# Two more pairs by seven: the first down groups of an FFN's second and third parts, and how their weights and left sides are summed

## The chip, the cores and the metric

The kernel runs on one core of one Trainium2 chip. The metric is the device time of one execution in microseconds (us). The engines are PE (TensorE, matmuls; PEld is its weight loads), DVE (VectorE), ACT (ScalarE), POOL (GpSimd, which here mostly issues DMAs) and SP (SyncE, which issues DMAs).

## The reference

One decoder block on 256 tokens with a model width of 2048, all in float32:

```
h = h + 1/2 * SwiGLU_a(RMSNorm(h))          # FFN1
n = RMSNorm(h); P = n @ W_in                # mixer
h = h + concat(GatedDeltaNet, StickBreaking) @ W_out
h = h + 1/2 * SwiGLU_b(RMSNorm(h))          # FFN2
h = h + sigmoid(RMSNorm(h) @ W_pg) * (p @ W_pp)
out = RMSNorm(h)

def swiglu(x, w_gu, w_down):
    gate, up = jnp.split(x @ w_gu, 2, axis=-1)
    return (jax.nn.silu(gate) * up) @ w_down        # w_gu 2048 x 11264, w_down 5632 x 2048
```

Only the two FFNs are touched by the change.

## The kernel before, in words

**Three matmuls for one.** Each operand is split in a high half (a cast to fp32r) and a low half (the residual), and a float32 product is made of hi x hi, hi x lo and lo x hi. A matmul here is always 128 x 128 (the left side, loaded as weights) by 128 x 512.

**Plain pairs.** Weights come in pairs of 128-row blocks (`weight_pair`, line 70 on): SP loads `raw` (512 KB), ACT casts `whi` (L77), DVE makes `wlo` (L78). One pair serves 2 blocks x 2 token halves x 3 = 12 matmuls (L550 to L552).

**Groups.** An FFN's 5632 hidden columns are eleven blocks of 512, in three parts: `PARTS = ((0, 3), (3, 7), (7, 11))`. Part one has three gate/up groups, then two down groups; parts two and three have four and two. In the code the parts are numbered 0, 1, 2, so part two's down weights are `w_down11` in FFN1. A group accumulates into four PSUM banks: two weight blocks by two token halves (a 2 x 2 product of blocks). A down group of part two or three has eight pairs for each of its two blocks.

**By seven.** The first `ns` pairs of a group are not multiplied plainly (24 matmuls for a pair of both blocks) but by seven products of a 2 x 2 scheme with 7 multiplications, 21 matmuls for a pair. The seven products belong to the next group but run inside the group before it, one after each plain pair ("sevenths"). Their weights are sums of four quarters, loaded by POOL into four banks `R` (L279): B11, B21, B12, B22 are `(0,0)`, `(1,0)`, `(0,1)`, `(1,1)`. `all_sums` forms the sums in place, either on DVE (`add`, L307) or by an accumulating DMA from POOL (`add_loaded`, L314); ACT casts each to `shi` (L298) and DVE makes the residual `slo` (L299). Two buffers of each exist. The products run in the order `SEVEN = (0, 1, 2, 4, 3, 5, 6)` (`product`, L342 to L344); numbers 0, 4 and 6 use plain left sides, 1, 2, 3 and 5 sums of them.

**Left sides.** The left sides of a down group are the hidden values `hTh`, `hTl`. `down_input` makes them after each gate/up group: `sil` is multiplied by the up product (DVE L482), transposed in squares (`tb`, L487), written to DRAM scratch (L493), read back as `tT` (L498) and split into `hTh` (ACT L504) and `hTl` (DVE L505). `halves` sums them for the products: one S of 512 columns for a pair (L456), four small operations of 128 columns (L462), then the cast `Sh` (ACT L464) and residual `Sl` (DVE L465). For parts two and three this is put in a lane after the sixth seventh of the second last gate/up group, one pair at a time.

**Order.** The program is written in the order of the lanes and groups; a scheduler reorders it within its own model, except for instructions marked `keep_in_program_order`. `next_weights` asks for weights two steps ahead. `last`, handed to `down_input` for a part's last block, is the number of steps (plain pairs) before the split of `tT` is issued.

Of the kernel before, what the change touches and what calls it, by code (L numbers as in the profile page):

```python
# [10 lines left out]
F32 = mybir.dt.float32  # L11
F32R = mybir.dt.float32r
AF = mybir.ActivationFunctionType
ALU = mybir.AluOpType
# [13 lines left out]


NS = 4  # L30
NS_DOWN = tuple(3 if i1 - i0 == 4 else 2 for i0, i1 in PARTS)


SEVEN = (0, 1, 2, 4, 3, 5, 6)


W_IN_ORDER = (2, 0, 4, 3, 1, 5, 8, 10, 12, 9, 11, 13, 6, 7)
# [9 lines left out]
def block_kernel(ctx, tc, a, out):  # L47
# [200 lines left out]
    class Group:  # L248
# [8 lines left out]
        def __init__(self, kind, part, src, quarters, ns, bank, nb=0):  # L257
            self.kind, self.part, self.src, self.ns, self.nb, self.bank = kind, part, src, ns, nb, bank
            self.quarters, self.raw, self.first = quarters, {}, False
            self.last = part == len(PARTS) - 1  # L260
            self.banks = self.follower = None
            self.plain = [(b, g) for b in range(2) for g in range(ns, len(src[0]))]
            if kind == "dn" and nb == 0:

                self.plain.sort(key=lambda x: x[1] >= len(src[0]) - 2)
            elif kind == "behind":

                self.plain.sort(key=lambda x: x[1] // 2)
            self.sums = self.all_sums()
# [11 lines left out]
        def loads(self, last=None):  # L281


            free = [last.home[q] for q in ((1, 0), (0, 1), (1, 1), (0, 0))] if last else ["R0", "R1", "R2", "R3"]
            self.queue = nc.gpsimd if last else nc.sync
            use = (0, 0), (0, 1), (1, 1), (1, 0)
            self.home = dict(zip(use, free))
            return [("load", lambda q=q: self.load(*q)) for q in use]

        def all_sums(self):  # L290

            fp = current[0]

            def halved(j, b):
                w = self.raw[j, b]
                hi = fp.tile([P, NS, NB], F32R, tag="shi", name="shi", bufs=2)[:, 0:self.ns]
                lo = fp.tile([P, NS, NB], F32R, tag="slo", name="slo", bufs=2)[:, 0:self.ns]
                keep(nc.scalar.copy(hi, w))  # L298
                nc.vector.tensor_tensor(out=lo, in0=w, in1=hi, op=ALU.subtract)  # L299
                return hi, lo  # L300

            def keep(ins):

                return tc.keep_in_program_order(ins) if self.first == "2" else ins

            def add(x, y):
                keep(nc.vector.tensor_tensor(out=self.raw[x], in0=self.raw[x], in1=self.raw[y], op=ALU.add))  # L307

            def add_loaded(x, y):


                if self.first:
                    return add(x, y)
                nc.gpsimd.dma_start(out=self.raw[x], in_=self.quarters[y[1]][y[0]], accum_op=ALU.add)  # L314
# [39 lines left out]
    def plan(n):  # L354
# [9 lines left out]
        for p, (i0, i1) in enumerate(PARTS):  # L364
            for i in range(i0, i1):
                plain = PLAIN[n]
                if i < plain:
                    src = [([a[f"w_gu{n}0"][2 * i + b][g] for g in range(KD // 2)], None) for b in range(2)]
                else:
                    src = [sources("w_gu" + n, 2 * (i - plain) + b) for b in range(2)]  # L370
                groups.append(Group("gu", p, [x[0] for x in src], [x[1] for x in src], NS if i >= plain else 0,
                                    len(groups) % 2))
            for nb in (0, 2):
                src = [sources(f"w_down{n}{p}", nb + b) for b in range(2)]
                groups.append(Group("dn", p, [x[0] for x in src], [x[1] for x in src], NS_DOWN[p], len(groups) % 2, nb))
# [47 lines left out]
    def halves(kind, his, los, ns, wait=0, at_once=2):  # L423


        for _ in range(wait):
            yield
# [12 lines left out]

        sides[kind] = side

        for g0 in range(0, ns, at_once):
            n = min(at_once, ns - g0)
            k0 = 2 * (g0 % 2)
            hi, lo = (x[g0 // 2][:, k0:k0 + 2 * n] for x in (his, los))
            keep = lambda ins: ins
            if g0 == 2 and n == 1:

                keep = tc.keep_in_program_order  # L450
                yield
            if n == 2:
                x = fp.tile([P, 2 * NB], F32, tag="sil", name="S")
            else:
                x = act.tile([P, NB], F32, tag="nat", name="S", bufs=4)
            keep(nc.vector.tensor_tensor(out=x, in0=hi.bitcast(F32).rearrange("p k x -> p (k x)"),  # L456
                                         in1=lo.bitcast(F32).rearrange("p k x -> p (k x)"), op=ALU.add))
            xv = x.rearrange("p (g j t y) -> p g j t y", g=n, j=2, t=2)
            a11, a12, a21, a22 = (xv[:, :, j, t, :] for t in range(2) for j in range(2))
            for o, y, z, op in ((a22, a21, a22, ALU.subtract), (a21, a11, a21, ALU.subtract),  # L460
                                (a11, a22, a11, ALU.subtract), (a12, a11, a12, ALU.add)):
                nc.vector.tensor_tensor(out=o, in0=y, in1=z, op=op)  # L462
            sx = [y[:, g0:g0 + n].rearrange("p g j t y -> p (g j t y)") for y in (sh, sl)]
            nc.scalar.copy(sx[0], x)  # L464
            nc.vector.tensor_tensor(out=sx[1], in0=x, in1=sx[0], op=ALU.subtract)  # L465
            if not g0 % 2 + n == 1 or g0 + n == ns:
                yield

    def ffn(n, nT, r, scale, next_norm, stat):
        xs = picker(*nT)  # L470
        late = callable(r)
        with tc.tile_pool(name="ffn", bufs=1) as fp:
            hTh, hTl = [], []

            def down_input(u, sil, th, tl, last):

# [24 lines left out]
                for t in range(2):  # L501
                    hi, lo = (x[:, :, t * P:(t + 1) * P].rearrange("p j (q y) -> p q j y", q=4) for x in (th, tl))
                    tv = tT[:, :, t].rearrange("p q (j y) -> p q j y", j=4)
                    keep(nc.scalar.copy(hi, tv))  # L504
                    keep(nc.vector.tensor_tensor(out=lo, in0=tv, in1=hi, op=ALU.subtract))  # L505

            def gated(g):
                sil = fp.tile([P, 2, NB], F32, tag="sil", name="sil")
# [7 lines left out]
            for group, todo in ffn_plan[n]:  # L516
# [5 lines left out]
                if dn and group.nb and not group.last:  # L522
                    lanes.add(1, halves("gu", *nT, NS))
                elif dn and group.nb and group.follower:
                    lanes.add(1, halves("behind", *nxt, NS_BEHIND, 4))
                elif not dn and group.follower.kind == "dn" and not group.part:
                    lanes.add(1, halves("dn", hTh[i0:], hTl[i0:], NS_DOWN[group.part]))
# [4 lines left out]
                for kind, one in todo:  # L532
                    if kind == "seventh":
                        follower = group.follower
                        follower.product(SEVEN[one])
                        if group.part and not dn and one == 5 and follower.kind == "gu" and \
                                follower.follower.kind == "dn":
                            p = PARTS[group.part][0]
                            lanes.add(1, halves("dn", Later(hTh, p), Later(hTl, p), NS_DOWN[group.part], 0, 1))
                        continue  # L540
                    b, g = one
                    whi, wlo = next_weights()
# [29 lines left out]
                    else:  # L572
# [776 lines left out]
def _layout(i):  # L1349
# [7 lines left out]
    for n in "12":  # L1357
# [4 lines left out]
        _parted(m, f"w_gu{n}", b[2 * PLAIN[n]:], NS)  # L1362
        b = _blocks(f[f"ffn{n}_w_down"][0])
        for p, (i0, i1) in enumerate(PARTS):
            _parted(m, f"w_down{n}{p}", b[:, 2 * i0:2 * i1], NS_DOWN[p])
# [32 lines left out]
```

## Time and profile before

| | us |
|---|---|
| three runs | 1946.11, 1944.25, 1944.34 |
| median | 1944.34 |
| profiled execution | 1945.28 |
| its span | 1943.6 |

The time of an execution is 1.7 us more than its span. In the profile's rows, a group of instructions has its busy time and the mean of one in ns; idle time in front of it is named with what ended it. In the table of stretches each engine has its busy time and the number of its instructions in that stretch; matmul ends are modelled, so PE's own busy time is always full there, and what it lost is seen from the number of its weight loads. In FFN1 part two's third gate/up group runs from 300.16 to 340.96 us, its last from 340.96 to 377.18, its two down groups from 377.18 to 465.21.

### The profile page before, as it was taken

Reading aid. Unit: us, or ns where it says so; the run is one execution under the profiler, and the core shown is the slowest. Engines: PE = TensorE matmul, PEld = TensorE weight load, DVE = VectorE, ACT = ScalarE, POOL = GpSimd, SP = SyncE. Lnnn points to the kernel's source line nnn. Section 1 sums busy time; section 2 is a strip of 40 time slices with the busy share of each in tenths; the row PEclk is TensorE's granted clock in tenths of the full one; section 3 lists DMA queues with packets and bytes.
Section 4 is the critical chain, followed back from the end, with each engine's and each line's share of the span. In section 5 each row is a group of like instructions: output and inputs, shape, how many; then the busy total and the mean of one; then the engine's idle time right before and its main releaser. Section 6 shows DMA issues by size and latency. Waiting matters only on the chain.

```text
span 1943.6 us, 24163 instructions
## 1 busy us (share of the span) xinstructions
PE 1928.1 (99%) x8884; PEld 1594.0 (82%) x8884; DVE 1570.4 (81%) x1703; ACT 1164.1 (60%) x1362; POOL 148.4 (8%) x226
## 2 busy tenths in 40 slices
PE   9999999999999999999999999999999999999998
PEld 7888888888888888878788888888888888888886
DVE  7879878997789766797856579899888987888865
ACT  6656666666666557664555456566556755657654
POOL 0010110000010000010100000010000100001000
PEclk9999999999999999999999999999999999999999
DMA  8778898888888765556565776788888987989764
GB/s 307 269 236 282 252 293 285 237 288 249 280 285 242 228 218 171 176 169 211 161 213 159 244 283 231 226 281 289 248 275 241 327 264 244 271 237 314 234 214 143
DMA packets 144182, 475.05 MB, mean 244 GB/s; under 512 B 19648, under 2 KB 47296, under 8 KB 129856
## 3 DMA queue, kind: packets, MB, share of 16 engines
q1 hardware_dynamic: 107200, 302.16, 44.4%
q0 software_dynamic: 25920, 160.44, 30.2%
q10 hardware_dynamic: 10944, 10.91, 1.8%
q8 instruction: 69, 1.13, 0.2%
q14 instruction: 49, 0.40, 0.1%
HBM read 451.44 MB, written 22.02 MB: 244 GB/s over the span
## 4 chain that ended last, share of the span: by engine, by line
PE 92%; DVE 5%; DMA 2%; issue 1%; ACT 0%; POOL 0%; SPq 0%; POOLq 0%; DVEq 0%; ACTq 0%
PE d L550 5%; PE d L552 5%; PE d L551 5%; PE u L551 5%; PE u L552 5%; PE u L550 5%; PE g L343 5%; PE g L342 5%; PE g L344 5%; PE g L551 4%; PE g L552 4%; PE pj L112 4%; PE pj L113 4%; PE pj L114 4%; PE g L550 4%; PE d L344 3%
## 5 line engine op out<-in xcount | busy, mean ns | idle before, releaser
L77 ACT CAST whi<-raw 128x1024 fp32r<-128x1024 f32 (+1 forms) x489 | 511.3, 1049 | 401.1 <-PE pj L114 106.6
L78 DVE TENSOR_TENSOR wlo<-raw,whi 128x1024 fp32r<-128x1024 f32 (+1 forms) x489 | 592.0, 1218 | 162.9 <-ACT whi L77 161.8
L299 DVE TENSOR_TENSOR slo<-R,shi 128x2048 fp32r<-128x2048 f32 (+2 forms) x224 | 444.9, 1989 | 132.1 <-ACT shi L298 130.1
L298 ACT CAST shi<-R 128x2048 fp32r<-128x2048 f32 (+2 forms) x224 | 373.9, 1671 | 141.5 <-DVE R L307 62.7
L112 PE MATMUL pj<-whi,nTh 128*128 128x512 f32 x448 | 179.4, 401 | 0.0
L113 PE MATMUL pj<-wlo,nTh 128*128 128x512 f32 x448 | 175.2, 391 | 1.1 <-DVE wlo L78 1.1
L114 PE MATMUL pj<-whi,nTl 128*128 128x512 f32 x448 | 174.9, 390 | 0.0
L550 PE MATMUL d<-whi,hTh 128*128 128x512 f32 x448 | 174.5, 390 | 0.0
L551 PE MATMUL d<-wlo,hTh 128*128 128x512 f32 x448 | 174.4, 389 | 0.0
L552 PE MATMUL d<-whi,hTl 128*128 128x512 f32 x448 | 173.4, 389 | 0.0
L551 PE MATMUL g<-wlo,nTh 128*128 128x512 f32 x400 | 156.6, 391 | 0.6 <-DVE wlo L78 0.6
L552 PE MATMUL g<-whi,nTl 128*128 128x512 f32 x400 | 156.0, 390 | 0.0
L551 PE MATMUL u<-wlo,nTh 128*128 128x512 f32 x400 | 155.8, 389 | 0.2 <-DVE wlo L78 0.2
L552 PE MATMUL u<-whi,nTl 128*128 128x512 f32 x400 | 155.6, 389 | 0.0
L550 PE MATMUL g<-whi,nTh 128*128 128x512 f32 x400 | 155.0, 391 | 0.6 <-ACT nTh L161 0.6
L550 PE MATMUL u<-whi,nTh 128*128 128x512 f32 x400 | 153.4, 389 | 0.0
L307 DVE TENSOR_TENSOR R<-R 128x2048 f32<-128x2048 f32 (+2 forms) x68 | 135.7, 1996 | 0.1
L113 PEld LDWEIGHTS pj<-wlo,nTh 128*128 128x128 f32 x448 | 84.2, 188 | 18.9 <-DVE wlo L78 2.7
L550 PEld LDWEIGHTS d<-whi,hTh 128*128 128x128 f32 x448 | 84.1, 188 | 18.1 <-ACT hTh L504 1.0
L552 PEld LDWEIGHTS d<-whi,hTl 128*128 128x128 f32 x448 | 84.1, 188 | 17.8
L114 PEld LDWEIGHTS pj<-whi,nTl 128*128 128x128 f32 x448 | 84.1, 188 | 17.6
L551 PEld LDWEIGHTS d<-wlo,hTh 128*128 128x128 f32 x448 | 84.1, 188 | 17.4
(332 smaller groups left out, 3447.0 us busy)
## 6 DMA issues: line engine op xcount, KB each, us to landing
raw<-in_w_gu SPq DMA_DIRECT2D x199, 512.0 KB, 5.8
raw<-in_w_down SPq DMA_DIRECT2D x112, 512.0 KB, 6.4
raw<-in_w_in SPq DMA_DIRECT2D x112, 512.0 KB, 3.4
R<-in_w_gu2q POOLq DMA_DIRECT2D x54, 1024.0 KB, 8.6
R<-in_w_gu1q POOLq DMA_DIRECT2D x48, 1024.0 KB, 8.3
raw<-in_w_out SPq DMA_DIRECT2D x32, 512.0 KB, 4.3
tT<-scr SPq DMA_DIRECT2D x22, 512.0 KB, 5.8
R<-in_w_down11q POOLq DMA_DIRECT2D x12, 768.0 KB, 7.0
```

The costliest lines, as they stand in the source:

```text
L77: nc.scalar.copy(hi[:, j, :], raw[:, j, :])
L78: nc.vector.tensor_tensor(out=lo[:, j, :], in0=raw[:, j, :], in1=hi[:, j, :], op=ALU.subtract)
L112: nc.tensor.matmul(outs[t], xh[:, c], whi[:, j, :], start=st, stop=False)
L113: nc.tensor.matmul(outs[t], xh[:, c], wlo[:, j, :], start=False, stop=False)
L114: nc.tensor.matmul(outs[t], xl[:, c], whi[:, j, :], start=False, stop=sp)
L298: keep(nc.scalar.copy(hi, w))
L299: nc.vector.tensor_tensor(out=lo, in0=w, in1=hi, op=ALU.subtract)
L307: keep(nc.vector.tensor_tensor(out=self.raw[x], in0=self.raw[x], in1=self.raw[y], op=ALU.add))
L344: nc.tensor.matmul(out, xl, whi[:, g, :], start=False, stop=sp, skip_group_check=True)
L550: nc.tensor.matmul(out, xh[:, c], whi[:, j, :], start=st, stop=False, skip_group_check=True)
L551: nc.tensor.matmul(out, xh[:, c], wlo[:, j, :], start=False, stop=False, skip_group_check=True)
L552: nc.tensor.matmul(out, xl[:, c], whi[:, j, :], start=False, stop=sp, skip_group_check=True)
```

## The change

For parts two and three, the first down group takes four pairs by seven instead of three; part two's second down group too, part three's second stays at three (`NS_DOWN`). In the first down groups, the product of A12 (number 4) comes second (`SEVEN_DOWN`), its quarter B21 is loaded second, and B11 + B12 is made by an accumulating DMA where DVE did it. The left sides of the first two pairs are summed in the gate/up group before (`first_sides`) and split directly after the sixth seventh; those of pairs two and three are summed straight from `tT` in `down_input`, behind its split, and split one step later; none is put in program order by itself except those in `down_input`. `last` falls from 3 to 2 where four pairs go by seven. `halves` is cut into functions for this.

```diff
-NS_DOWN = tuple(3 if i1 - i0 == 4 else 2 for i0, i1 in PARTS)
+NS_DOWN = (2, 2), (4, 4), (4, 3)
...
+SEVEN_DOWN = (0, 4, 1, 2, 3, 5, 6)
...
+            self.seven = SEVEN_DOWN if kind == "dn" and part and nb == 0 else SEVEN
...
-            use = (0, 0), (0, 1), (1, 1), (1, 0)
+            use = ((0, 0), (0, 1), (1, 1), (1, 0)) if self.seven is SEVEN else ((0, 0), (1, 0), (0, 1), (1, 1))
...
-            for i in SEVEN:
+            for i in self.seven:
...
                 if i == 0:
-                    add((0, 0), (0, 1))
+                    (add if self.seven is SEVEN else add_loaded)((0, 0), (0, 1))
                     add_loaded((0, 1), (1, 1))
...
+            def first_sides(p0):
+                for _ in range(4):
+                    yield
+                for g in range(2):
+                    x = act.tile([P, NB], F32, tag="nat", name="S", bufs=4)
+                    sum_sides(x, hTh[p0:], hTl[p0:], g)
+                    early.append(x)
+                    yield
+
+            def later_sides(s, made):
+                yield
+                for g, x in made:
+                    split_sums(s, g, x)
...
+                if pending:
+                    s, ns = pending.pop()
+                    made = []
+                    for g in range(2, ns):
+                        x = act.tile([P, NB], F32, tag="nat", name="S", bufs=4)
...
+                        add_sides([xv[:, j, t] for t in range(2) for j in range(2)],
+                                  [tT[:, :, t, 32 * (k + j):32 * (k + j) + 32] for t in range(2) for j in range(2)],
+                                  keep)
+                        made.append((g, x))
+                    lanes.add(1, later_sides(s, made))
...
+                elif not dn and group.part and group.follower.kind == "gu" and group.follower.follower.kind == "dn":
+                    lanes.add(1, first_sides(i0))
...
-                            lanes.add(1, halves("dn", Later(hTh, p), Later(hTl, p), NS_DOWN[group.part], 0, 1))
+                            lanes.finish(1)
+                            s = left_sides("dn", Later(hTh, p), Later(hTl, p))
+                            for g in range(2):
+                                split_sums(s, g, early.pop(0))
+                            pending.append((s, NS_DOWN[group.part][0]))
...
-                        last = (3 if i1 - i0 == 4 else 2) if len(hTh) == i1 else 0
+                        last = (6 - NS_DOWN[group.part][0] if i1 - i0 == 4 else 2) if len(hTh) == i1 else 0
```

What this moves, at three places in FFN1's part two. The lines of the changed file are its own (L301 is `slo`, L309 the sum on DVE, L316 the accumulating DMA, L456 the small left side sums, L448 `Sl`, L594 to L596 the plain matmuls). First, DVE in the last gate/up group. Before, from the second product's residual on (`R_2548` is the bank of B11):

```order
L299 TENSOR_TENSOR slo_2728<-R_2548,shi_2727 128x1536
L487 STREAM_TRANSPOSE tb_2744<-sil_2526 128x4x128
L307 TENSOR_TENSOR R_2548<-R_2548,R_2625 128x1536
L487 STREAM_TRANSPOSE tb_2744<-sil_2526 128x4x128
L78 TENSOR_TENSOR wlo_2749<-raw_2747,whi_2748 128x1024
L456 TENSOR_TENSOR S_2770<-hTh_2382,hTl_2383 128x512
L299 TENSOR_TENSOR slo_2793<-R_2548,shi_2792 128x1536
```

And after, from the residual of the quarter B21 on, which is now second:

```order
L301 TENSOR_TENSOR slo_2738<-R_2590,shi_2737 128x2048
L456 TENSOR_TENSOR S_2714<-S_2714,tT_2610 128x128
L79 TENSOR_TENSOR wlo_2758<-raw_2756,whi_2757 128x1024
L513 STREAM_TRANSPOSE tb_2753<-sil_2526 128x4x128 x2
L448 TENSOR_TENSOR Sl_2678<-S_2709,Sh_2677 128x512
L448 TENSOR_TENSOR Sl_2678<-S_2714,Sh_2677 128x512
L301 TENSOR_TENSOR slo_2801<-R_2548,shi_2800 128x2048
L79 TENSOR_TENSOR wlo_2807<-raw_2805,whi_2806 128x1024
L309 TENSOR_TENSOR R_2548<-R_2548,R_2645 128x2048
L79 TENSOR_TENSOR wlo_2842<-raw_2840,whi_2841 128x1024
L301 TENSOR_TENSOR slo_2836<-R_2548,shi_2835 128x2048
```

A quarter that needs no sum stands ahead of the first sum's residual (`slo_2801`), the splits of two left sides stand in front of it, and the one DVE sum left stands between it and the next residual.

Second, POOL's DMAs for that group's products. Before:

```order
L279 DMA R_2548<-in_w_down11q 128x1536
L279 DMA R_2584<-in_w_down11q 128x1536
L279 DMA R_2625<-in_w_down11q 128x1536
L279 DMA R_2633<-in_w_down11q 128x1536
L314 DMA R_2584<-in_w_down11q 128x1536
L314 DMA R_2548<-in_w_down11q 128x1536
```

After:

```order
L281 DMA R_2548<-in_w_down110q 128x2048
L281 DMA R_2590<-in_w_down110q 128x2048
L281 DMA R_2637<-in_w_down110q 128x2048
L316 DMA R_2637<-in_w_down110q 128x2048
L281 DMA R_2645<-in_w_down110q 128x2048
L316 DMA R_2548<-in_w_down110q 128x2048
```

The row that accumulates into `R_2548` for the first sum is the last of these; before, the sum into that bank was DVE's `L307`, and the same accumulating DMA served only the third sum. The last load of a quarter now stands behind an accumulating DMA.

Third, PE where a part's last block (`hTh_2992` before, `hTh_3016` after) is first read in the first down group. Before, 117 matmuls behind the group's first one:

```order
L342 MATMUL d1_3061<-shi_3141,Sh_2683 128x512
L343 MATMUL d1_3061<-slo_3142,Sh_2683 128x512
L344 MATMUL d1_3061<-shi_3141,Sl_2684 128x512
L550 MATMUL d0_2778<-whi_3148,hTh_2992 128x512
L551 MATMUL d0_2778<-wlo_3149,hTh_2992 128x512
```

After, 86 behind it:

```order
L345 MATMUL d1_3088<-slo_3105,Sh_2677 128x512
L346 MATMUL d1_3088<-shi_3104,Sl_2678 128x512
L345 MATMUL d0_3087<-slo_3141,hTh_2085 128x512
L594 MATMUL d0_2783<-whi_3110,hTh_3016 128x512
L595 MATMUL d0_2783<-wlo_3111,hTh_3016 128x512
```

The block is read 31 matmuls sooner, since two of the plain pairs that stood ahead of it have gone by seven.

In the whole program there are 18 matmuls less: in each FFN 21 more in the last gate/up groups of parts two and three each, 24 less and 21 more in part two's first down group, 24 less in its second, and 24 less in part three's first. Of the residuals `slo`, 14 instead of 56 have 1536 columns and 175 instead of 133 have 2048; of the DVE sums, 4 instead of 16 and 50 instead of 42; `wlo` and `whi` are 12 fewer; POOL's DMAs are four more, all accumulating.

More of the change, by code (lines that the diff above doesn't have):

```diff
@@ L421, in block_kernel, with left_sides @@
     order.append(("pair", a["w_pp"][3]))
-    def halves(kind, his, los, ns, wait=0, at_once=2):
-        for _ in range(wait):
-            yield
+    def left_sides(kind, his, los):
         fp = current[0]
@@ L441, in halves @@
         sides[kind] = side
[L443 to L467, printed above, removed]
@@ new lines, in sum_sides, with halves @@
+    def sum_sides(x, his, los, g0):
+        n = x.shape[1] // NB
+        k0 = 2 * (g0 % 2)
+        hi, lo = (y[g0 // 2][:, k0:k0 + 2 * n].bitcast(F32).rearrange("p k x -> p (k x)") for y in (his, los))
+        nc.vector.tensor_tensor(out=x, in0=hi, in1=lo, op=ALU.add)
+        xv = x.rearrange("p (g j t y) -> p g j t y", g=n, j=2, t=2)
+        xs = [xv[:, :, j, t, :] for t in range(2) for j in range(2)]
+        add_sides(xs, xs)
+    def halves(kind, his, los, ns, wait=0):
+        for _ in range(wait):
+            yield
+        s = left_sides(kind, his, los)
+        for g0 in range(0, ns, 2):
+            x = current[0].tile([P, 2 * NB], F32, tag="sil", name="S")
+            sum_sides(x, his, los, g0)
+            split_sums(s, g0, x)
+            yield
@@ L472, in ffn @@
         with tc.tile_pool(name="ffn", bufs=1) as fp:
[L473 removed]
+            hTh, hTl, early, pending = [], [], [], []
+            def first_sides(p0):
[5 more added lines that the diff above has]
+                    early.append(x)
+                    yield
+            def later_sides(s, made):
+                yield
+                for g, x in made:
+                    split_sums(s, g, x)
             def down_input(u, sil, th, tl, last):
@@ L534, in ffn @@
                         follower = group.follower
-                        follower.product(SEVEN[one])
+                        follower.product(follower.seven[one])
                         if group.part and not dn and one == 5 and follower.kind == "gu" and \
```

24 lines of the change are left out of this document (20 added, 4 removed).

## The prediction

> **What bounds the kernel now.** I read the page's head, the clock row and the chain first, then the waits of the TensorE (PE), then a table of stretches around the edit.
>
> ```profile
> span 1943.6 us, 24163 instructions
> PE 1928.1 (99%) x8884; PEld 1594.0 (82%) x8884; DVE 1570.4 (81%) x1703; ACT 1164.1 (60%) x1362; POOL 148.4 (8%) x226
> PEclk9999999999999999999999999999999999999999
> PE 92%; DVE 5%; DMA 2%; issue 1%; ACT 0%; POOL 0%; SPq 0%; POOLq 0%; DVEq 0%; ACTq 0%
> PE vp L1129 <- DVE R L1150: 1.2, 1, 1.2
> PE g L551 <- DVE wlo L78: 0.6, 2, 0.4
> PE u L343 <- DVE slo L299: 0.3, 1, 0.3
> ```
>
> PE is busy 99% of the span at full clock and is 92% of the chain; its largest single wait is 1.2 us; the only one for a product's weight (slo) is 0.3. So the kernel is bound by the number of matmuls, and VectorE (DVE, 81% on average) matters only where it delivers a weight or a left side too late. Whether it can is a question for each stretch. Part two's groups are these (the first row is its third gate/up group, the second its last, the third and fourth the beginning and the whole of its two down groups); the last three rows are the last gate/up groups of part three and, in FFN2, of parts two and three.
>
> ```profile
> core 0: us, PE busy (x) PEld busy (x) DVE busy (x) ACT busy (x) POOL busy (x), PEclk, DMA share, GB/s
> 300.16:340.96 40.80, 40.80 (x182) 33.78 (x180) 35.46 (x28) 24.05 (x21) 3.95 (x6) 1.00 0.85 261
> 340.96:377.18 36.22, 36.22 (x161) 29.75 (x159) 32.71 (x41) 23.71 (x27) 3.96 (x6) 1.00 0.81 237
> 377.18:421.00 43.82, 43.82 (x195) 36.30 (x194) 42.01 (x41) 27.92 (x27) 4.84 (x7) 1.00 0.92 301
> 377.18:465.21 88.03, 88.03 (x388) 72.48 (x387) 80.21 (x70) 51.96 (x48) 8.01 (x13) 1.00 0.87 283
> 587.61:623.87 36.26, 36.26 (x160) 29.77 (x159) 32.71 (x41) 23.71 (x27) 3.96 (x6) 1.00 0.82 238
> 1483.66:1519.90 36.24, 36.24 (x160) 29.74 (x159) 32.71 (x41) 23.71 (x27) 3.93 (x6) 1.00 0.80 238
> 1730.34:1766.60 36.26, 36.26 (x160) 29.77 (x159) 32.71 (x41) 23.71 (x27) 3.91 (x6) 1.00 0.83 240
> ```
>
> The weight loads (PEld) count the matmuls best. The first row has 180 in 40.80 us: 0.2267 us each, the price of a matmul with nothing late. By that price the second row should take 159 x 0.2267 = 36.04 us and takes 36.22, so 0.18 us were lost; the last three lose 0.22, 0.20 and 0.22. The two down groups lose 88.03 - 387 x 0.2267 = 0.30. DVE is busy 90% of the last gate/up group, 96% of 377 to 421 and 91% of both down groups, and PE still loses almost nothing there.
>
> **The change, part by part.**
>
> *Matmuls.* One more pair by seven takes two plain pairs of 12 matmuls out of its group and puts 21 into the group before. Part two's last gate/up group gets +21, its first down group -24 +21 (the second has one more pair too), its second -24: -6. Part three: +21 and -24: -3. Nine for each FFN, 18 in all: 18 x 0.2267 = **-4.08 us**. The Trainium skill, "TensorE: Matmul & The Clock Gate", section "Back-to-back issue gap", gives about 131 ns for a matmul of 512 columns in a sustained stream with weight loads and about 216 ns for one alone; by these the term would be 2.4 or 3.9 us. The trace's 226.7 ns disagrees with the first and decides.
>
> *Idle time that can go.* The four last gate/up groups grow by 21 matmuls (36.2 to 41.0 us). What DVE has there is dearer by the piece, but there is more time. These are the prices.
>
> ```profile
> L78 DVE TENSOR_TENSOR wlo<-raw,whi 128x1024 fp32r<-128x1024 f32 x87 | 105.4, 1219 | 11.6 <-ACT whi L77 11.4
> L299 DVE TENSOR_TENSOR slo<-R,shi 128x2048 fp32r<-128x2048 f32 x34 | 77.9, 2291 | 32.3 <-ACT shi L298 32.2
> L299 DVE TENSOR_TENSOR slo<-R,shi 128x1536 fp32r<-128x1536 f32 x28 | 48.9, 1754 | 5.1 <-ACT shi L298 5.1
> L307 DVE TENSOR_TENSOR R<-R 128x2048 f32<-128x2048 f32 x10 | 22.8, 2276 | 0.0
> L307 DVE TENSOR_TENSOR R<-R 128x1536 f32<-128x1536 f32 x8 | 14.0, 1746 | 0.0
> L462 DVE TENSOR_TENSOR S<-S 128x128 f32<-128x128 f32 x24 | 6.5, 290 | 0.1
> L465 DVE TENSOR_TENSOR Sl<-S,Sh 128x512 fp32r<-128x512 f32 x6 | 4.1, 691 | 1.4 <-ACT Sh L464 1.4
> L456 DVE TENSOR_TENSOR S<-hTh,hTl 128x512 f32<-128x512 f32 x6 | 4.1, 688 | 0.0
> L298 ACT CAST shi<-R 128x2048 fp32r<-128x2048 f32 x34 | 65.1, 1913 | 31.3 <-DVE R L307 16.3 <-PE g L344 9.0 <-PE u L344 5.0
> ```
>
> A residual of four pairs costs 2.29 instead of 1.75 us (+0.54), a sum 2.28 instead of 1.75 (+0.53). In part two's last gate/up group: seven residuals +3.8, the sum +0.5; of the left sides there are now 8 small sums and two splits, where 10 small, two large and three splits stood, -2.6. DVE comes to 34.4 of 41.0 us, 84% instead of 90%. The group before gets one large sum, six small ones, two splits and a dearer residual, +4.4, and loses a DVE sum, -1.75: 38.1 of 40.8 us, 93% instead of 87%, no more than what 377 to 421 bears. With the lower share in the last groups I take the 0.18 + 0.22 + 0.20 + 0.22 as gone: **-0.8 us**; the other end is that it stays (0).
>
> *The first sum by DMA.* The bank of B11 may be written only after its residual is done, then an accumulating DMA adds B12, then follow cast, residual, DVE sum with B22, cast and residual.
>
> ```profile
> 337.23 1.76 DVE L299 TENSOR_TENSOR slo<-R,shi 128x1536 fp32r<-128x1536 f32 x1 [0.50 <-ACT shi L298]
> 341.16 0.89 POOL L314 DMA_DIRECT2D R<-in_w_down11q  x1 [5.33 <-DVE S L462]
> L314 POOL DMA_DIRECT2D R<-in_w_down11q x4: 877/881/885, 341.2 to 392.7; - x4
> DMA to landing us min/median/max: 5.5/8.5/11.9
> ```
>
> The last two rows are of that line's accumulating DMAs: part two's of FFN1, and the time to landing of all. The first residual ended at 338.99; with 0.54, two splits (0.69 each) and two small sums (0.29 each) ahead of it, it ends near 341.5. POOL is free by then (its last issue before is the one at 341.16). The DMA, at the median of 8.5 us, lands at 350.0; 1.91 + 2.29 give the residual at 354.2 (PE uses it 73 matmuls into the group, 340.96 + 16.5 = 357.5); the sum, the cast and the last residual take 2.28 + 1.91 + 2.29, with one or two plain residuals (1.22) between: 361.9 to 363.1. PE wants it 100 matmuls in: 363.6. So 0.5 to 1.7 us are left at the median; at 11.9 it is 1.7 to 2.9 late, at 5.5 in time by 3.5. I take **+0.1** for each of four groups.
>
> *The down groups begin with later blocks.* With pairs 0 to 3 gone, the first plain pair reads the part's third block (before: 12 matmuls into the group), and its low half is read 14 matmuls after the start instead of 20.
>
> ```profile
> 374.88 1.49 ACT L298 CAST shi<-R 128x1536 fp32r<-128x1536 f32 x1 [2.12 <-PE d L344]
> 376.40 1.76 DVE L299 TENSOR_TENSOR slo<-R,shi 128x1536 fp32r<-128x1536 f32 x1
> 378.74 1.75 DVE L307 TENSOR_TENSOR R<-R 128x1536 f32<-128x1536 f32 x1
> 380.40 1.29 DVE L505 TENSOR_TENSOR hTl<-tT,hTh 128x512 fp32r<-128x512 f32 x2
> 381.71 0.39 PE L552 MATMUL d<-whi,hTl 128*128 128x512 f32 x1
> 382.74 1.30 DVE L487 STREAM_TRANSPOSE tb<-sil 128x512 f32<-128x512 f32 x2
> 384.07 2.06 SPq L493 DMA_DIRECT2D scr<-tb  x4
> 390.53 0.33 SPq L498 DMA_DIRECT2D tT<-scr  x1
> DMA to landing us min/median/max: 5.9/5.9/5.9
> 399.08 1.29 DVE L505 TENSOR_TENSOR hTl<-tT,hTh 128x512 fp32r<-128x512 f32 x2
> ```
>
> Call the start of the down groups D (377.18). Before, hTl ended at 381.05 and 381.69, read at 381.71. That cast waited for the end of the product two before. In the changed order that product ends 24 matmuls, 5.4 us, before D, so cast, residual, sum and the sil and hTl pairs, packed, end at about D + 3.0 and D + 3.6; read at D + 3.2 and D + 3.9. That is 0.2 early, or 0.9 late with a plain residual between: **+0.1** each.
>
> The last block is read 86 matmuls after D (19.5 us) instead of 117 (26.5). Before, its transposes ended at D + 6.9, and tT landed at 390.53 + 5.9 = D + 19.3. From transposes ended to landed is thus 12.4 us. Now the transposes can end between D + 4.9 (straight behind hTl at D + 3.6) and D + 7.9 (as before, with the sum and the residual dearer), tT lands at D + 17.3 to D + 20.3, and the high half, a copy as long as one part of hTl (0.65), is there at D + 17.9 to D + 20.9: 1.6 us early to 1.4 late. Near the middle, **+0.1** each. SP issues the tT load behind plain weights, six fewer for part two, so it is not later there.
>
> *DVE in part two's two down groups.* Seven residuals +0.54, two sums +0.53, four plain residuals less (1.22 each, -4.9): 80.2 + 3.8 + 1.1 - 4.9 = 80.2 us, while the time falls by 27 matmuls to 81.9: 98%. The first half had 96% and lost under 0.1. **+0.1** for each FFN; the other end is the second rival.
>
> *The rest* lies beside PE: four accumulating DMAs more (0.89 us of issue each on a POOL that is 8% busy), ACT's larger casts (ACT is busy 59% of the down groups), the weight layout, the pinning that is dropped. If DMA share, 0.92 at 377 to 421, became the cover that is gone, a late plain weight costs at first the 0.2 to 0.4 of the two waits in the list.
>
> Sum: -4.08 - 0.8 + 4 x 0.3 + 0.2 = **-3.5 us**. The profiled execution took 1945.28, 0.94 over the median; the other two runs lie at 1944.3, so I put the sum on the median 1944.34: **1940.8**. A difference under 0.2% (3.9 us) is one that a measurement of this kernel can hardly tell; faster begins at 1940.45. The forecast is beside that line.
>
> **The rivals.**
>
> 1. *Nothing waits, and the stretches lose less than now.* For it: 96% DVE at 377 to 421 with almost no loss. All of the 0.8, the 0.3 of part two's down groups in both FFNs go too: -4.08 - 1.4 = -5.5, **1938.9**.
> 2. *DVE becomes the bound in part two's down groups* (slower). Of those 88.03 us it had 7.8 idle, part of it in waits for a cast, which waits for a product that frees its buffer. If these 7.8 stay, the stretch takes 80.2 + 7.8 = 88.0 instead of 81.9 us: 6.1 late, twice, less the 4.08: +8.1, **1952.5**. It decides from 2.0 us per FFN (no gain); slower by 0.2% from 4. Against it: DVE's idle time there is largely slack, since PE did not wait. The Trainium skill, "Perfetto Trace Analysis", section "Identifying the Most-Contended Engine", takes the engine with the highest occupancy for the bound and weight-load time, not matmul time, for TensorE; by that, 72.5 us of weight loads stand against 80.2 of DVE, and this change would load the wrong engine. The 0.30 us lost there speak against it.
> 3. *The chains by DMA come late*: the accumulating DMA near its longest, 1.7 at each of four groups, or the last block 1.4 at each, less what is in the sum: 4 x 1.4 = -3.5 + 5.6 would be slower, but such landings are the ends; half of them gives +0.7 x 4 = 2.8: **1943.6**, no change. For it: in the first stretch the DMA queues are 85% busy.
>
> **How the numbers follow.** The sum 0.62, its own range 1939.4 (half of the small waits, more idle gone) to 1942.2 (idle stays, half as much again late), 0.28 of it faster than the line. Rival 1 0.16, all faster. Rival 3 0.13, nearly all no change. Rival 2 0.09, slower. So faster 0.44, same 0.47, slower 0.09. The range leaves out the second rival and the upper end of the third: 1938.9 to 1943.4.
>
> **What would show it.** Weight loads of the two downs of part two 360 in about 81.9 us, of the last gate/up groups 180 in 40.8 to 41.1 us. Right: no PE wait on slo, hTh or hTl over 0.3 us. Wrong: PE waits on d <- DVE slo or wlo in part two's downs (rival 2), or on hTh/hTl some 20 us after D, or on the third product in the last gate/up group with DVE idle <- POOL just ahead (rival 3).

## The result, and the profile after

The changed kernel takes 1965.5 us (median of 4 runs, 1963.0 to 1969.4), the kernel before 1944.3 (1944.12 to 1946.11). The ratio is 1.011, with a 95% interval of 1.0096 to 1.0123: 21 us slower, where 3.5 us faster was forecast, with a range that ended at 1943.4. The profiled execution, whose trace is read below, took 1963.0 us and was the shortest of the four. One execution of a version below (e4), 7352 us at a granted clock of 0.445, is left out of that version's interval.

Head of the page after, with the first line of its chain:

```profile
span 1961.3 us, 24097 instructions
PE 1932.2 (99%) x8866; PEld 1593.5 (81%) x8866; DVE 1578.9 (81%) x1703; ACT 1171.5 (60%) x1354; POOL 151.9 (8%) x230
PE 82%; DVE 8%; DMA 4%; issue 4%; ACT 1%; ACTq 0%; POOL 0%; SPq 0%; DVEq 0%; POOLq 0%
```

The 18 matmuls are gone (8884 to 8866), but PE makes up 82% of the chain and no longer 92%, and DMA is in it with 4% where it had 2%. PE's own busy share still reads 99%: it does not show the loss. Its waits do (what it waited for: us in total, times, the longest):

```profile
PE d L345 <- DVE slo L301: 12.7, 5, 2.9
PE d L344 <- ACT shi L300: 1.7, 2, 1.1
```

Before, no wait of this kind was over 0.3 us. I laid the starts of consecutive matmuls side by side and counted what lies over 226.7 ns (called the excess below). Nearly all of it is in one place four times: the last gate/up group of parts two and three, in both FFNs, 4.5, 6.1, 4.8 and 5.7 us, 21.1 in all. In part two's down groups and part three's first there are 0.4 to 0.6 us each, 2.1 in all, at places where before there was none. With -4.1 for the matmuls this gives +19, against a last matmul that comes 17.6 us later in the profiled execution (the rest is small differences elsewhere).

The chain of waits through part two's last gate/up group in FFN1 names the way (start, us, what; ... marks rows left out). It is the story of the third product, B11 + B12:

```profile
341.44 12.46 DMA R<-in_w_down110q
354.13 0.31 ACTq L519
...
356.07 0.35 ACT Sh L447
356.62 0.43 issue
357.05 2.28 DVE slo L301
359.40 0.98 issue
360.38 2.30 DVE R L309
362.78 1.92 ACT shi L300
364.73 2.30 DVE slo L301
```

The accumulating DMA is issued at 341.44 and lands 12.46 us later. It does not come by itself; POOL's timeline has two transfers close ahead of it, the other accumulating DMA and the last quarter's load:

```profile
334.58 0.89 POOL L316 DMA_DIRECT2D R<-in_w_down110q  x1 [5.21 <-DMA R<-in_w_down110q]
335.34 0.67 POOL L281 DMA_DIRECT2D R<-in_w_down110q  x1
341.44 0.88 POOL L316 DMA_DIRECT2D R<-in_w_down110q  x1 [5.43 <-issue]
```

The load was still in flight until 347.59, and the other accumulating DMA until 342.93. Of the 64 accumulating DMAs in this trace only the four first sums in question were issued with two others of POOL's DMAs in flight, and they are the four slowest, 12.4 to 14.0 us; none of the other 60, and none of the 60 in the trace before, had more than one in flight or took over 11.9 us.

Then comes a second delay. The cast that waits for the DMA stands on ACT ahead of the cast of a left side and of the DMAs that ACT issues, and none of them starts before it. ACT's timeline, then DVE's:

```profile
353.98 1.91 ACT L300 CAST shi<-R 128x2048 fp32r<-128x2048 f32 x1 [5.09 <-DMA R<-in_w_down110q]
354.13 1.94 ACTq L519 DMA_DIRECT2D scr<-tb  x4
355.79 0.61 ACT L447 CAST Sh<-S 128x512 fp32r<-128x512 f32 x1
```

```profile
356.44 0.69 DVE L448 TENSOR_TENSOR Sl<-S,Sh 128x512 fp32r<-128x512 f32 x1 [5.14 <-ACT Sh L447]
357.05 2.28 DVE L301 TENSOR_TENSOR slo<-R,shi 128x2048 fp32r<-128x2048 f32 x1
```

DVE, which is the busiest engine beside PE in these groups, stands idle for 5.14 us because the Sh that it wants waits on ACT behind a cast for another operand. The residual starts at 357.05, 1.16 us after its own cast has ended, and PE gets it at 359.39 where it wanted it at 356.5. So of the 2.9 us at this product the late landing alone makes some 1.7, and the wait behind the left side 1.2; this is worked out from the rows, and no run separates the two.

Last, in three of the four places PE's clock was lowered as well. PE's timeline in part three of FFN1, and two stretches of the table by stage (the last figure but two is the granted clock):

```profile
607.65 0.50 PE L344 MATMUL d<-shi,Sh 128*128 128x512 f32 x1 [1.05 <-ACT shi L300]
611.10 0.80 PE L345 MATMUL d<-slo,Sh 128*128 128x512 f32 x1 [2.95 <-DVE slo L301]
611.69 0.63 PE L346 MATMUL d<-shi,Sl 128*128 128x512 f32 x1
612.12 0.63 PE L344 MATMUL d<-shi,Sh 128*128 128x512 f32 x1
```

```profile
611.10:613.20 2.10, 2.10 (x5) 1.72 (x6) 2.10 (x2) 0.00 (x0) 0.00 (x0) 0.50 0.03 8
359.50:362.00 2.50, 2.50 (x11) 2.05 (x12) 2.50 (x2) 0.00 (x0) 0.00 (x0) 1.00 0.19 45
```

After the wait in part three the matmuls start 0.43 us apart at a clock of 0.50; after the one in part two, at 1.00, 0.23 to 0.24.

### The profile page after: what moved, and what is told of

The parts are those of the page before. It is cut to its first block, busy times and chain, and to the rows that moved or that the text cites. A ratio compares the mean times of both kernels' runs of the same rounds, so it can differ in the third digit from the quotient of the medians.

```text
span 1961.3 us, 24097 instructions
## 1 busy us (share of the span) xinstructions
PE 1932.2 (99%) x8866; PEld 1593.5 (81%) x8866; DVE 1578.9 (81%) x1703; ACT 1171.5 (60%) x1354; POOL 151.9 (8%) x230
## 4 chain that ended last, share of the span: by engine, by line
PE 82%; DVE 8%; DMA 4%; issue 4%; ACT 1%; ACTq 0%; POOL 0%; SPq 0%; DVEq 0%; POOLq 0%
PE d L594 4%; PE d L596 4%; PE d L595 4%; PE pj L113 4%; PE g L345 4%; PE g L346 4%; PE pj L114 4%; PE g L344 4%; PE pj L115 4%; PE u L594 4%; PE u L595 4%; PE u L596 4%; PE g L595 3%; PE g L596 3%; PE g L594 3%
## 5 line engine op out<-in xcount | busy, mean ns | idle before, releaser
L78 ACT CAST whi<-raw 128x1024 fp32r<-128x1024 f32 (+1 forms) x477 | 499.2, 1050 | 391.2 <-PE pj L115 105.9
L79 DVE TENSOR_TENSOR wlo<-raw,whi 128x1024 fp32r<-128x1024 f32 (+1 forms) x477 | 578.3, 1218 | 160.5 <-ACT whi L78 159.3
L301 DVE TENSOR_TENSOR slo<-R,shi 128x2048 fp32r<-128x2048 f32 (+2 forms) x224 | 467.4, 2089 | 122.9 <-ACT shi L300 119.5
L300 ACT CAST shi<-R 128x2048 fp32r<-128x2048 f32 (+2 forms) x224 | 392.0, 1751 | 181.1 <-DVE R L309 86.5
L594 PE MATMUL d<-whi,hTh 128*128 128x512 f32 x400 | 156.1, 391 | 0.0
L596 PE MATMUL g<-whi,nTl 128*128 128x512 f32 x400 | 155.8, 389 | 0.0
L596 PE MATMUL u<-whi,nTl 128*128 128x512 f32 x400 | 155.7, 389 | 0.0
L594 PE MATMUL g<-whi,nTh 128*128 128x512 f32 x400 | 155.6, 391 | 0.0
L595 PE MATMUL d<-wlo,hTh 128*128 128x512 f32 x400 | 155.5, 389 | 0.0
L596 PE MATMUL d<-whi,hTl 128*128 128x512 f32 x400 | 155.2, 390 | 0.0
L594 PE MATMUL u<-whi,nTh 128*128 128x512 f32 x400 | 154.8, 390 | 0.0
L309 DVE TENSOR_TENSOR R<-R 128x2048 f32<-128x2048 f32 (+2 forms) x64 | 133.2, 2080 | 0.2
L115 PEld LDWEIGHTS pj<-whi,nTl 128*128 128x128 f32 x448 | 84.1, 188 | 17.6
L113 PEld LDWEIGHTS pj<-whi,nTh 128*128 128x128 f32 x448 | 84.2, 188 | 16.6
L345 PE MATMUL g<-slo,nTh 128*128 128x512 f32 x234 | 91.4, 390 | 0.0
L346 PE MATMUL g<-shi,nTl 128*128 128x512 f32 x234 | 91.2, 390 | 0.0
```

The costliest lines, as they stand in the source:

```text
L78: nc.scalar.copy(hi[:, j, :], raw[:, j, :])
L79: nc.vector.tensor_tensor(out=lo[:, j, :], in0=raw[:, j, :], in1=hi[:, j, :], op=ALU.subtract)
L113: nc.tensor.matmul(outs[t], xh[:, c], whi[:, j, :], start=st, stop=False)
L115: nc.tensor.matmul(outs[t], xl[:, c], whi[:, j, :], start=False, stop=sp)
L345: nc.tensor.matmul(out, xh, wlo[:, g, :], start=False, stop=False, skip_group_check=True)
L346: nc.tensor.matmul(out, xl, whi[:, g, :], start=False, stop=sp, skip_group_check=True)
```

## The experiments

**The first sum on DVE again (e1).** The theory (A): the DMA of the first sum is late, and that is the loss. The rival (B): the left sides, summed and split elsewhere, are late.

```diff
-                    (add if self.seven is SEVEN else add_loaded)((0, 0), (0, 1))
+                    add((0, 0), (0, 1))
```

> The changed kernel with one thing undone: in the first down groups of parts two and three B11 + B12 is again summed by DVE and not by an accumulating DMA. Theory A (the accumulating DMA of the first sum lands 12 to 14 us after its issue, not 8.5, and the third product waits for it): the waits of d on slo and shi in the four last gate/up groups (some 20 us in the changed kernel's excess over 226.7 ns a matmul) go almost wholly, DVE's share of those groups rises by one sum of 2.3 us, and the time is 1939.5 to 1942. Rival B (the left sides of pairs two and three, cast and split late and in front of the residual on DVE, are what is late): they stay, DVE has 2.3 us more, and the time is 1960 or more.

Measured: 1945.06 us, ratio to before 1.0004 (0.9995 to 1.0014). Twenty of the 21 us go with this one line, with the left sides as in the change. So A, not B. The gain does not come, though: no difference from before, and 3 us over the upper end of what A expected. The trace has 5.2 us of new excess at places where before has none, against 4.1 us of matmuls: 0.49 us at the fourth product in each of the four last gate/up groups, 1.26 and 0.84 in part two's down groups and 0.57 twice in part three's first. PE's waits in FFN1's part two, 340 to 410 us, are these:

```profile
PE d L594 <- ACT hTh L530: 0.5, 1, 0.5
PE d L345 <- DVE slo L301: 0.2, 1, 0.2
PE d L344 <- ACT part L352: 0.2, 1, 0.2
```

The first is the part's last block; the third is a product that must wait until ACT has copied its bank (a wait listed as 0.2 goes with 0.49 us of excess, since the matmuls just behind a wait also start further apart). DVE's timeline shows what stands ahead of the block's transposes, and ACT's the cast at the end:

```profile
382.50 2.28 DVE L309 TENSOR_TENSOR R<-R 128x2048 f32<-128x2048 f32 x1
384.70 1.29 DVE L531 TENSOR_TENSOR hTl<-tT,hTh 128x512 fp32r<-128x512 f32 x2
385.91 1.22 DVE L79 TENSOR_TENSOR wlo<-raw,whi 128x1024 fp32r<-128x1024 f32 x1
387.04 1.30 DVE L513 STREAM_TRANSPOSE tb<-sil 128x512 f32<-128x512 f32 x2
```

```profile
402.65 1.14 ACT L530 CAST hTh<-tT 128x512 fp32r<-128x512 f32 x2 [0.61 <-DMA tT<-scr]
```

From the end of the transposes (388.34) to the cast, which waited for the landing, it is 14.3 us through the DRAM scratch, where before it was 12.4 to the landing. SP issues the load of `tT` 7.9 us after the transposes (at 396.19) and not 6.5 as before, and it takes 6.4 us and not 5.9.

**POOL's order alone (e4).** The DMA stays, but the second bank's accumulating DMA is issued behind it (`add_loaded` has a third argument here, which pins the DMA in program order; its own lines are left out):

```diff
                 if i == 0:
                     (add if self.seven is SEVEN else add_loaded)((0, 0), (0, 1))
-                    add_loaded((0, 1), (1, 1))
+                    if self.seven is SEVEN:
+                        add_loaded((0, 1), (1, 1))
+                elif i == 4 and self.seven is not SEVEN:
+                    add_loaded((0, 1), (1, 1), tc.keep_in_program_order)
```

> The changed kernel, the DMA kept, with POOL's order changed alone: the accumulating DMA of the second bank (B12 += B22) is issued behind that of the first sum and not ahead of the last quarter's load. Theory A1 (the first sum's DMA is slow because it shares the queue with that accumulating DMA and the last load): it lands 8 to 10 us after its issue and not 12.5 and 14.0, some 3 to 4 us sooner, and of the 4.5 to 6 us lost in each of the four groups 1 to 2 are left: 1943 to 1950. Theory A2 (whatever lies beside it, an accumulating DMA issued there takes 12 us or more, since the plain weights and the last load keep the engines full): it lands as late as before and the time stays at 1961 to 1967.

Measured: 1947.97 us, 1.0018 (1.0008 to 1.0028). Issue to landing of the same transfer in this kernel, and PE's waits on hTl and slo:

```profile
DMA to landing us min/median/max: 8.9/8.9/8.9
```

```profile
PE d L599 <- DVE hTl L534: 2.7, 3, 1.5
PE d L348 <- DVE slo L301: 1.4, 4, 0.7
```

8.9 us instead of 12.5 (in part three 8.0 instead of 14.0), and 17 us of the loss are gone: A1. The last quarter's load has landed before the issue here, or 0.3 us behind it. That the DMA is slow is thus not its own length but what is in flight ahead of it. The other transfer pays: issued right behind, it takes 14.6 us itself, and a new wait of 0.7 to 1.7 us on the third block's hTl appears in three of the four places.

**The order undone too (e3).** A11, then the first sum, on DVE; four pairs and new left sides as in the change.

```diff
-            self.seven = SEVEN_DOWN if kind == "dn" and part and nb == 0 else SEVEN
+            self.seven = SEVEN
```

> The changed kernel with the DMA and the order undone (A11, then the first sum, as in the kernel before; B11 + B12 on DVE); the four pairs and the new left sides stay. Theory A: the order matters little once the sum is on DVE: 1939.5 to 1943. Rival C (with four pairs the old order's second product is late, since sum, cast and residual of 2.3 + 1.9 + 2.3 us lie between two products 5.4 us apart, which A12's product gives room for): 1 to 3 us lost in each of four groups, 1944 to 1952.

Measured: 1949.69 us, 1.0025 (1.0015 to 1.0034): rival C's loss, but not quite at its place. It is the third product that waits, not the second, 1.2 us in each of the four groups (1.5 to 1.7 with the matmuls just behind it):

```profile
PE d L344 <- ACT shi L300: 4.2, 4, 1.0
```

ACT's and DVE's timelines, two rows of each below, show a longer way than the 6.5 us that I had put down: from the first sum's cast (ACT, 344.51) to the second's (353.43) it is 8.9 us, since the residual between them, ready to go at 346.4, stood behind hTl, left sides and one plain residual on DVE and started at 348.71.

```profile
344.51 1.91 ACT L300 CAST shi<-R 128x2048 fp32r<-128x2048 f32 x1
...
353.43 1.90 ACT L300 CAST shi<-R 128x2048 fp32r<-128x2048 f32 x1
```

```profile
348.71 2.28 DVE L301 TENSOR_TENSOR slo<-R,shi 128x2048 fp32r<-128x2048 f32 x1
...
351.11 2.28 DVE L309 TENSOR_TENSOR R<-R 128x2048 f32<-128x2048 f32 x1
```

**The same with three pairs (e5).** `NS_DOWN = (2, 2), (3, 3), (3, 3)` in the kernel just told.

> The kernel of e3 (old order, B11 + B12 on DVE, the new left sides) with three pairs by seven in each down group of parts two and three, as before the change: as many matmuls as before. Theory A with the chain (in e3 the third product waits 1.2 us in each of four groups because from one sum to the next cast, residual and sum take 1.9 + 2.3 + 2.3 = 6.5 us where two products start 5.4 us apart; with three pairs it is 1.5 + 1.75 + 1.75 = 5.0): no wait of d on shi over 0.2 us is left there and the time is that of before, 1943.5 to 1945.5. Rival (the new, unpinned left sides in front of the residuals are what makes the third product late): the four waits stay and the time is 1947 to 1950.

Measured: 1944.69 us, 0.9999 (0.999 to 1.0009), and no excess over 0.2 us at any one place in these groups. The wait belongs to the fourth pair. Whether to the longer pieces or to the fourth pair's left side, which goes with it, this run does not tell apart.

**The DMA alone in the kernel before (b1).** Three pairs, old order, old left sides; only the first sum of the first down groups is an accumulating DMA.

```diff
-                    add((0, 0), (0, 1))
+                    (add_loaded if self.kind == "dn" and self.part and self.nb == 0 else add)((0, 0), (0, 1))
```

> The kernel before with one thing of the change alone: in the first down groups of parts two and three (three pairs by seven, old order, old left sides) B11 + B12 is made by an accumulating DMA. Theory A: the DMA lands 8 to 12 us after the first residual, and the second product, which is wanted 48 matmuls into the last gate/up group, waits 2 to 5 us for it in each of four groups: 1952 to 1965. Rival B (the left sides are what is late in the changed kernel): under 1 us for each, 1943 to 1947.

Measured: 1960.85 us, 1.0092 (1.0075 to 1.0109): A again, in a kernel with none of the rest. What waits here I had not expected: for the larger part it is not the product but the plain matmuls.

```profile
PE g L551 <- DVE wlo L78: 9.7, 6, 2.4
PE d L343 <- DVE slo L299: 3.0, 3, 1.3
```

```profile
349.76 1.47 ACT L298 CAST shi<-R 128x1536 fp32r<-128x1536 f32 x1 [5.94 <-DMA R<-in_w_down11q]
351.14 1.99 ACT L77 CAST whi<-raw 128x1024 fp32r<-128x1024 f32 x2
```

The DMA (768 KB here, again with two others of POOL's in flight ahead of it) took 8.7 to 10.7 us in the four places. ACT stands for 5.94 us at the cast that wants the sum, and two casts of plain weights come after it in one go. DVE stands for 5.55 us at the residual behind that cast, and makes the plain `wlo` after it only at 355.84. So the late DMA stops a stream that has nothing to do with it.

**The DMA in part three alone (e6).** e1's edit for part two only.

> The changed kernel with B11 + B12 on DVE again in part two alone; in part three it stays a DMA. If the two parts' losses are separate and due to that DMA: part two's last gate/up groups lose about 0.5 each as in e1, part three's about 6 each as in the changed kernel, and the time is e1's 1945.1 + 2 x 5.5 = 1956, between 1954 and 1958. The first matmuls behind the wait of over 3 us run at half rate again (0.43 us instead of 0.227). If instead the parts disturb one another, the time lies outside.

Measured: 1956.62 us, 1.0064 (1.0047 to 1.0081), 11.6 us over e1 where 11 were expected: the parts add up. Part two's groups lose 0.49 each, part three's 5.8 and 7.1, with the slow matmuls behind each.

**The DMA with the old order (e7).**

```diff
-SEVEN_DOWN = (0, 4, 1, 2, 3, 5, 6)
+SEVEN_DOWN = (0, 1, 2, 4, 3, 5, 6)
...
-            use = ((0, 0), (0, 1), (1, 1), (1, 0)) if self.seven is SEVEN else ((0, 0), (1, 0), (0, 1), (1, 1))
+            use = (0, 0), (0, 1), (1, 1), (1, 0)
...
-                    (add if self.seven is SEVEN else add_loaded)((0, 0), (0, 1))
+                    (add_loaded if self.kind == "dn" and self.part and self.nb == 0 else add)((0, 0), (0, 1))
```

> The changed kernel with the old order of products (A12's fourth) and of loads, the DMA kept: the first sum is wanted by the second product, 24 matmuls (5.4 us) sooner than in the changed kernel. Theory A: what the four groups lose grows by most of 5.4 us each, less what the lead now hides: from about 5.2 to 8 to 11 us each: 1975 to 1990. Rival (the wait is set by the left sides, split behind the cast that waits, and not by when the sum is wanted): 1963 to 1968, as the changed kernel.

Measured: 1976.56 us, 1.0167 (1.0152 to 1.0183). So it counts when the sum is wanted, and the rival is out. The four groups lose 8.7, 6.8, 8.1 and 9.4 us, 33 in all, 12 more than in the changed kernel. That is 3 us a group, less than the 5.4 us by which A12's place moves the want; in part, the DMA lands sooner with the old order of loads (after 12.4, 10.7, 11.1 and 12.2 us).

```profile
PE d L344 <- ACT shi L300: 16.2, 4, 4.8
PE d L345 <- DVE slo L301: 4.5, 4, 1.2
```

**Where e1's gain went (e8, e9).** Two versions of e1 with fewer fourth pairs: none, `(3, 3), (3, 3)`, and part two's alone, `(4, 4), (3, 3)`.

> The kernel of e1 (A12's product second, B11 + B12 on DVE, new left sides) with three pairs by seven in each down group of parts two and three: as many matmuls as before the change. e1 loses 0.49 us at the fourth of these products in each of four groups (a wait for ACT's copy of the bank, L352) and 0.3 to 0.9 on hTh of the last block in each part. If the longer pieces (casts and residuals of four pairs) and the earlier need of the last block make these, both are gone: 1943.5 to 1945. If the order makes the first (A12 second puts two products on one bank next to each other), four times about 0.5 stays without any gain: 1946 to 1947.

Measured: 1944.39 us, 0.9998 (0.9989 to 1.0007). None of e1's waits is there, at the fourth product either; the largest excess at one place is 0.2 us. A12 second costs nothing with three pairs.

> The kernel of e1 with part three's first down group back at three pairs: part two's four pairs alone, 12 matmuls (2.7 us) less than before the change where e1 has 18 (4.1 us). If each piece pays its matmuls and costs the small waits seen in e1's trace at its own place, part three's 0.49 and 0.57 us in each FFN go (2.1 us) and 1.4 us of matmuls come back: e1's 1945.1 falls to about 1944.4, no difference from before; the trace shows no excess over 0.2 us at part three's last block. If the waits belong to something else (the left sides, the order), they stay and the time is 1946 or more.

Measured: 1944.1 us, 0.9996 (0.9987 to 1.0006), as expected. The trace has part two's excess (0.49 and 0.8 in each FFN) and none of part three's. Each fourth pair thus pays 3 matmuls, 0.68 us, and costs 0.65 to 1.1 us: 1.3 to 1.75 for part two's two in an FFN, 1.06 for part three's one (e1, e9). No version that I ran beats the kernel before by more than the measurement can tell.

## Why the prediction was wrong

*Matmuls, -4.08: right.* 18 fewer, and 226.7 ns is still the spacing of matmuls wherever nothing is late.

*The first sum by DMA, +0.1 for each group: the step that failed.* The groups lost 4.5 to 6.1 us each, and 0.49 once the sum was on DVE again (e1). The issue was forecast at 341.5 and came at 341.44 (in part by luck, since the group itself began 1 us sooner than before, and PE wanted the residual 1 us sooner too); the landing at 350.0 came at 353.9, and the end of the residual at 354.2 came at 359.3. Two things were missing. I took the median landing of all accumulating DMAs, 8.5 us, and for the end of the range the longest, 11.9. But I had the order of the queue in front of me, in which two transfers of 1 MB stand directly ahead: POOL was free to issue, as I wrote, but its transfers were not done, and in the trace before no accumulating DMA was issued behind two others in flight. In the four places it took 12.5, 14.0, 12.4 and 13.6 us. And I followed the chain of this operand only, cast, residual, sum, and did not ask what stands behind the waiting cast on ACT. There the late DMA held Sh, and through Sh DVE, which stood for 5.1 us.

*The third rival* named the mechanism, this DMA near its longest. It gave it 0.13 and then halved its price, because "such landings are the ends". All four were beyond the end. The sign it gave, a wait of PE on the third product, is what came, though DVE stood for ACT just ahead of it and not for POOL. Its price for the worst case, 1.7 to 2.9 us a group, was too low too: it counted only the last sum of the chain, while PE waited for the first sum, then for the next (1.3 us more in part two), and in three places lost clock. (Its -3.5 + 5.6, called slower there, is 2.1 us, which is less than the 3.9 us that the prediction itself calls hard to tell.)

*Idle time that can go, -0.8: it went, but other waits hid it.* The starts of matmuls before show 159 matmuls in each of the four last gate/up groups and 0.17 to 0.22 us of excess, 0.14 of it at one plain pair (353.45 us in part two of FFN1). In e5 and e8, with as many matmuls as before, these groups have under 0.04 us, and in the changed kernel there is nothing at that pair. In e1 it is part of why 5.2 us of new excess against 4.1 us of matmuls cost only 0.5 us.

*The last block, +0.1 each: right mechanism, mis-sized.* It cost 0.3 to 0.8 in each part in e1, within my bounds of 1.6 early to 1.4 late; the way through the scratch took 14.3 us and not 12.4, in which SP's issue was 1.4 us later although I had written that it would not be. *The third block's residual, +0.1: right.* It cost 0.1 in each of the four groups of the changed kernel; it grew in e4 when another transfer was in its way.

*DVE as the bound in part two's downs (second rival): no.* In e1 these groups lose 0.8 and 1.3 us, where the rival had 6.1. About half of it is the last block; the other half, 0.5, is a wait on a residual, as the rival has it. The weight-load rule of the Trainium skill that I set beside this rival, "Perfetto Trace Analysis", section "Identifying the Most-Contended Engine", would have been of no help here: the engine that the loss ran through was ACT, busy 60% of the span.

## What to carry to other kernels

Before work is moved from a busy engine to a DMA, look up what is in flight at the moment of its issue and take the landing from rows with that company, not a median; and ask what stands behind the first instruction that will wait for it, on its engine. Here a cast on an engine that is 60% busy held up DVE, the plain weights and PE. A saving of a few matmuls at a time (0.68 us here) is only as good as the slack of each chain it shortens, and the busy shares of the engines over the whole span give no hint of that slack.

## What the runs showed of the hardware

A long wait of PE has a second price. Counted from start to start over 226.7 ns, waits of 2.48 to 2.88 us (five, in the changed kernel and in the DMA alone in the kernel before) left the following matmuls at full speed. Nine of 3.14 to 4.97 us (changed kernel, e6, e7) went with matmuls 0.43 us apart at a clock of 0.50. That cost 1.4 to 2.4 us more in the changed kernel and e6, and 3.4 to 4.6 in e7, with a second wait in it. The Trainium skill, "TensorE: Matmul & The Clock Gate", section "Why this matters for your kernels", advises no idle gaps over about 3 us between bursts of matmuls; these traces agree with it as a rule of thumb.

The length of one wait is not the whole of it, though. In the second place of e6 the clock fell while PE had stood only 1.1 us of its wait, with another wait of 1.28 us shortly before; in part two of the changed kernel a wait of 2.72 us (as listed) did not lower it. Two stretches of e6 and two of the changed kernel show it (PE's busy time comes second, the clock is the last figure but two):

```profile
1750.45:1753.86 3.41, 1.05 (x4) 0.31 (x2) 1.08 (x2) 3.25 (x3) 0.00 (x0) 1.00 0.99 376
1753.86:1755.70 1.84, 0.00 (x0) 0.00 (x0) 1.84 (x2) 0.00 (x0) 0.00 (x0) 0.50 0.23 68
354.66:358.07 3.41, 2.01 (x9) 1.31 (x7) 1.63 (x2) 2.69 (x3) 0.00 (x0) 1.00 1.01 402
358.07:361.48 3.41, 2.09 (x9) 1.73 (x10) 3.41 (x3) 0.00 (x0) 0.00 (x0) 1.00 0.22 75
```

By the clock records of the traces, the clock of the changed kernel falls at 610.66, 1511.78 and 1764.36 us, 264 and 74 steps of 3.413 us apart, and each time for one step (in e6 and e7 for one to three). Cut by such steps, all eleven traces agree: in the step before each of the nine falls PE stood for 1.96 us or more, and in no other step at full clock between 20 and 1930 us for more than 1.76. So in these traces it is the idle time within one step that goes with the fall, and whether a wait of 2 to 3 us is charged may depend on where it lies. No run moves a wait on purpose to test that.

Two accumulating DMAs of 1 MB issued back to back took 8.9 and 14.6 us (e4), and the first of them took 12.5 us in the changed kernel, behind the other and a load: the order of issue decides who waits. In the four places of the changed kernel it landed 6.1 to 6.4 us after the load ahead of it.
